# A weight sum in a tile of its own for the second quad of an up-projection on Trainium2

## Chip, core and metric

The kernel runs on one core of one Trainium2 chip. The metric is the device time of one execution in microseconds (us); the time given for a kernel is the median of several executions. TensorE (PE) multiplies, ScalarE (ACT) and VectorE (DVE) prepare and finish tiles, GpSimd (POOL) and SyncE (SP) issue the transfers (DMAs) that matter here; a transfer that adds to what its target holds (accumulating) is issued by POOL, a plain load by SP.

## The reference

One decoder layer on 512 tokens of width 1024, in float32. The part around the change is its last third, a gated MLP with hidden width 2816:

```python
def conv_gated_mlp(x, w_up, conv_w, conv_b, w_down):
    h = x @ w_up                                   # 512x1024 @ 1024x5632
    h = causal_depthwise_conv(h, conv_w, conv_b)   # width 3
    gate, val = jnp.split(h, 2, axis=-1)
    return (jax.nn.silu(gate) * val) @ w_down      # 512x2816 @ 2816x1024

# in the layer, after the mixers (SSD and forgetting attention) and their output projection:
hf = rms_norm(x, norm_ffn_w)
x = x + conv_gated_mlp(hf, w_up, ffn_conv_w, ffn_conv_b, w_down)
```

## The kernel before

**Products.** Every float32 operand is split into a high part (`wh`, `uh`, `sh`, rounded to the multiplier's format) and a low part (`wl`, `ul`, `sl`, what is left), and a product is three matmuls: high by high, high by low, low by high (`mm3`, line 110). A weight tile of 128x1024 is split by one cast on ACT and one subtraction on DVE (`split_up`, line 929); TensorE reads the results.

**Quads.** The up-projection is cut into 11 quads. A quad is 512 output columns: four quarters B11, B12, B21, B22 of the weights, each 128x1024 float32 (512 KB), by two halves of the tokens (H1, H2). Quad 0 is computed plainly (`plain`, `tokens`). From quad 1 on, seven products do the work of eight. Product 0 (`n0`) multiplies B11, product 2 (`n2`) B11+B12, product 3 (`n3`, the fourth) B11+B12+B22, product 4 (`n4`) the sum of all four, product 1 B21, product 5 B22, product 6 B22+B12. One product is 24 matmuls with 256 columns.

**Sums of weights.** They are made by transfers. SP loads B11 into the tile `Ta` (`load_a`, line 995). When it has been split for product 0, POOL adds B12 to it (`more`, line 985, an accumulating transfer); when that has been split for product 2, POOL adds B22; after the split for product 3, B21. So `Ta` holds the four sums one after another, and each addition waits for the split of the sum before it. `Tb` is likewise B22 for product 5 and then B22+B12 for product 6. B21 comes into a tile `wraw` (`Tb` lies in buffers of the same tag). Tiles of tag `T` lie in a pool of two buffers, used in turn, except for every third quad, whose `Ta` has a buffer of its own.

**Quad 1 is special.** It is set up while quad 0 is still being computed, before the loop over `quad_step` starts. Its `Ta` is loaded and gets B12 at once (lines 1352 to 1356); product 0 reads B11 from a second copy, `T0` (line 1358). Then stand, in code order, products 0, 1, 2, 5, the weights of product 0 of quad 2, the weights and product 3, and the weights of product 6. `quad_step(1)` follows: it computes what is left of quad 1 (products 6 and 4) together with products 0, 2, 1, 5 and 3 of quad 2.

**Order.** Each engine and each queue runs its instructions strictly in order; a waiting instruction holds those behind it. The order is set when the kernel is built, by a scheduler with priorities and by explicit "not before" dependencies (`in_turn`, `ordered`, `issue_after`). An accumulating transfer that adds to a tile waits, on POOL, until the earlier transfer into that tile has landed.

**After product 3** ACT copies its result out of PSUM (`n3_kept`, tile `y3`, line 979), since product 6 adds to the same bank. In ACT's order the cast for product 6 (of `Tb`) stands ahead of this copy, and the cast for product 2 of quad 2 behind it.

Of the kernel before, what the change touches and what calls it, by code (L numbers as in the profile page):

```python
# [8 lines left out]
F32 = mybir.dt.float32  # L9
# [6 lines left out]
P = 128  # L16
# [23 lines left out]
def tile_hybrid_layer(  # L40
# [18 lines left out]
    nc = tc.nc  # L59
# [15 lines left out]
    def raw(ap):  # L75
        return ap.bitcast(F32)
# [727 lines left out]
    B11, B12, B21, B22 = 0, 1, 2, 3  # L804
    ADD, SUB = ALU.add, ALU.subtract

    ptt = ctx.enter_context(tc.tile_pool(name="ptt", bufs=1, side="right", reuse_waits="tile"))
# [111 lines left out]
    def ordered(high, low):  # L919
        for name, ins, first in zip(("h", "l"), (high, low()), taken.get(made[0] - 4, (None, None))):  # L920
            in_turn(name, ins)
            if first is not None:
                dep = mybir.DependencyInfo(mybir.DependencyClass.NoSync, mybir.DependencyReason.DATA)
                tc.add_manual_dep(ins.ins, first.ins.name, dep, reason="issue_after")
        made[0] += 1

    def split_up(r, where=None):
        h, l = where or [wp.tile([P, 1024], F32R, tag=t, name=t, bufs=3) for t in ("wh", "wl")]
        ordered(act.copy(h, r), lambda: dve.tensor_tensor(out=l, in0=r, in1=raw(h), op=SUB))  # L929
        return h, l  # L930
# [5 lines left out]
    def pair(n):  # L936
        if FROM[n] not in pairs:
            return None
        pairs[n] = pairs.pop(FROM[n])
        return pairs[n]  # L940
# [7 lines left out]
    quads = [Quad() for _ in range(NH)]  # L948
# [35 lines left out]
    def more(t, quarter, q):  # L984
        last_more[0] = nc.gpsimd.dma_start(t, wup[quarter, q], accum_op=ALU.add)  # L985
# [24 lines left out]
    def n2_weights(q):  # L1010
        u = quads[q]
        u.w2 = split_up(u.ta, pair("n2"))
        more(u.ta, B22, q)

    def n3_weights(q):
        u = quads[q]
        u.w3 = split_up(u.ta, pair("n3"))
        more(u.ta, B21, q)

    def n4_weights(q):  # L1020
        quads[q].w4 = split_up(quads[q].ta, pair("n4"))
# [20 lines left out]
    def n0(q, where=None):  # L1042
        if not hasattr(quads[q], "w0"):
            n0_weights(q, where)
        n0_product(q)
        with urgent():
            n0_kept(q)
# [25 lines left out]
    def n2(q):  # L1073
        n2_weights(q)
        n2_product(q)
        with urgent():
            n2_kept(q)
# [8 lines left out]
    def n3(q):  # L1086
        n3_weights(q)
        n3_product(q)
        with urgent():
            n3_kept(q)  # L1090
# [124 lines left out]
    T = []  # L1215
# [23 lines left out]
    def quad_step(q, ahead=None):  # L1239
# [8 lines left out]
        dve_turn(n1_added(q))  # L1248
        dve_turn(low12(q))
        n2_weights(n)  # L1250
        n0_kept(n)
        n5_weights(n)
# [18 lines left out]
        gate_bias(q)  # L1271
        gate_taps(q, 0)
        n3_weights(n)
        n1_product(n)
        gate_taps(q, 1)
# [10 lines left out]
    def spare():  # L1286
        return [pa.tile([P, 1024], F32R, tag=t, name=t, bufs=1) for t in ("wh", "wl")]
# [68 lines left out]
    tc.add_manual_dep(last_more[0].ins, normed.ins.name, dep, reason="issue_after")  # L1356
    quads[1].t0 = ptt.tile([P, 1024], F32, tag="T", name="T0", bufs=2)
    nc.sync.dma_start(quads[1].t0, wup[B11, 1])
    tokens(1)
    n0(1, spare())  # L1360
    n1_weights(1)
# [5 lines left out]
    pairs.update(n2=four[0], n4=four[3], n1=four[1], n5=four[2])  # L1367
    n0_weights(2)
    n3_weights(1)
    n3_product(1)  # L1370
    n6_weights(1)
# [17 lines left out]
    q = NH - 1  # L1389
# [278 lines left out]
```

## Time and profile before

| | |
|---|---|
| median of 3 runs | 762.45 us (761.83, 762.45, 769.46) |
| profiled execution, its own time | 762.75 us |
| span of the profiled execution | 761.0 us |
| PE busy | 754.4 us (99% of the span) |
| DVE, ACT, POOL busy | 599.3, 487.9, 204.4 us |
| DMA, mean rate over the span | 148 GB/s, 112.91 MB |

The span is from the first to the last instruction; 1.75 us of the profiled execution's own time lie outside it. Times in rows are us from the span's start. A row of the timeline gives start, duration, engine, line, operation, output and input, the count of instructions that were merged into it, and in brackets how long the engine sat idle before it and what ended that. The weights of quad 1 are made from 420 to 485 us; quads 1 to 9 then pass in steps of about 19 us up to 650 us, and the down-projection ends the kernel.

### The profile page before, as it was taken

Reading aid. Unit: us, or ns where it says so; the run is one execution under the profiler, and the core shown is the slowest. Engines: PE = TensorE matmul, PEld = TensorE weight load, DVE = VectorE, ACT = ScalarE, POOL = GpSimd, SP = SyncE. Lnnn points to the kernel's source line nnn. Section 1 sums busy time; section 2 is a strip of 40 time slices with the busy share of each in tenths; the row PEclk is TensorE's granted clock in tenths of the full one; section 3 lists DMA queues with packets and bytes.
Section 4 is the critical chain, followed back from the end, with each engine's and each line's share of the span. In section 5 each row is a group of like instructions: output and inputs, shape, how many; then the busy total and the mean of one; then the engine's idle time right before and its main releaser. Section 6 shows DMA issues by size and latency. Waiting matters only on the chain.

```text
span 761.0 us, 12538 instructions
## 1 busy us (share of the span) xinstructions
PE 754.4 (99%) x4647; PEld 652.2 (86%) x4647; DVE 599.3 (79%) x965; ACT 487.9 (64%) x870; POOL 204.4 (27%) x254
## 2 busy tenths in 40 slices
PE   9999999999999999999999999999999999999997
PEld 7888888887888778787777899999999999888886
DVE  5797788578577676579695787988888888999885
ACT  6655767764379687685673665766666666666551
POOL 0001013445273553134200011333333333223120
PEclk9999999999999999999999999999999999999999
DMA  9534233242254242434221437888888888689992
GB/s 334 181 107 148 84 111 113 83 139 83 85 166 137 58 153 81 127 108 143 84 83 57 166 64 153 193 198 194 194 193 196 193 195 193 179 225 210 252 184 92
DMA packets 35085, 112.91 MB, mean 148 GB/s; under 512 B 4176, under 2 KB 5264, under 8 KB 35024
## 3 DMA queue, kind: packets, MB, share of 16 engines
q1 hardware_dynamic: 23744, 73.58, 28.6%
q0 software_dynamic: 10848, 38.02, 27.4%
q8 instruction: 36, 0.59, 0.3%
q10 hardware_dynamic: 432, 0.52, 0.2%
q14 instruction: 25, 0.20, 0.1%
HBM read 106.24 MB, written 2.20 MB: 142 GB/s over the span
## 4 chain that ended last, share of the span: by engine, by line
PE 98%; DMA 1%; DVE 1%; SPq 0%; issue 0%; ACT 0%; DVEq 0%
PE G L110 19%; PE pw L110 17%; PE g L110 13%; PE Z L110 13%; PE po L110 12%; PE Y L110 5%; PE X L110 4%; PE o L687 2%; PE pT L674 2%; PE y L501 2%; PE j L110 1%; PE S L652 1%; PE S L651 1%; PE qkT L601 1%; DMA wr<-in_wxbc_dram 1%; PE st L523 1%
## 5 line engine op out<-in xcount | busy, mean ns | idle before, releaser
L110 PE MATMUL pw<-wl,xh 128*128 128x512 f32 x192 | 75.8, 395 | 0.0
L110 PE MATMUL pw<-wh,xh 128*128 128x512 f32 x192 | 75.5, 397 | 0.0
L110 PE MATMUL pw<-wh,xl 128*128 128x512 f32 x192 | 75.4, 394 | 0.0
L97 DVE TENSOR_TENSOR wl<-wraw,wh 128x1024 fp32r<-128x1024 f32 x51 | 63.4, 1246 | 8.8 <-ACT wh L96 8.6
L110 PE MATMUL G<-uh,wh 128*128 128x256 f32 x256 | 70.3, 276 | 0.0
L110 PE MATMUL G<-ul,wh 128*128 128x256 f32 x256 | 70.3, 276 | 0.0
L110 PE MATMUL G<-uh,wl 128*128 128x256 f32 x256 | 69.2, 276 | 0.0
L96 ACT CAST wh<-wraw 128x1024 fp32r<-128x1024 f32 x51 | 53.7, 1056 | 14.1 <-PE g L110 5.4
L110 PE MATMUL g<-xh,wh 128*128 128x512 f32 x144 | 56.7, 393 | 0.7 <-ACT wh L188 0.7
L110 PE MATMUL g<-xl,wh 128*128 128x512 f32 x144 | 56.8, 394 | 0.0
L110 PE MATMUL g<-xh,wl 128*128 128x512 f32 x144 | 56.5, 393 | 0.0
L985 POOL DMA_DIRECT2D Ta<-in_wup_dram x30 | 26.2, 875 | 108.6 <-DVE wl L929 106.2
L657 ACT ACTIVATE prob<-prob,nm 128x128 f32<-128x128 f32 (+1 forms) x64 | 35.8, 561 | 27.9 <-DVE nm L653 27.6
L653 DVE CUSTOM_DVE_ANT_0 prob<-S,prob 128x128 f32<-128x128 f32 (+1 forms) x64 | 30.0, 486 | 27.6 <-PE S L652 27.4
L1236 ACT CAST wh<-T 128x1024 fp32r<-128x1024 f32 (+1 forms) x32 | 31.5, 985 | 29.9 <-DMA T<-in_wdown_dram 8.0
L110 PEld LDWEIGHTS G<-ul,wh 128*128 128x128 f32 x256 | 48.1, 188 | 0.0
L110 PEld LDWEIGHTS G<-uh,wh 128*128 128x128 f32 x256 | 48.1, 188 | 0.0
L929 DVE TENSOR_TENSOR wl<-Ta,wh 128x1024 fp32r<-128x1024 f32 x39 | 47.4, 1217 | 0.7 <-ACT wh L929 0.6
L110 PEld LDWEIGHTS G<-uh,wl 128*128 128x128 f32 x256 | 47.4, 188 | 0.0
L1236 DVE TENSOR_TENSOR wl<-T,wh 128x1024 fp32r<-128x1024 f32 (+1 forms) x32 | 36.4, 1137 | 11.5 <-ACT wh L1236 11.4
L110 PE MATMUL G<-sh,wh 128*128 128x256 f32 x160 | 44.2, 276 | 0.0
L110 PE MATMUL G<-sl,wh 128*128 128x256 f32 x160 | 44.2, 276 | 0.0
(305 smaller groups left out, 2421.1 us busy)
## 6 DMA issues: line engine op xcount, KB each, us to landing
Ta<-in_wup_dram POOLq DMA_DIRECT2D x30, 512.0 KB, 5.5
T<-in_wdown_dram POOLq DMA_DIRECT2D x23, 512.0 KB, 7.1
wraw<-in_wqk_dram SPq DMA_DIRECT2D x16, 512.0 KB, 3.6
wraw<-in_wout_dram SPq DMA_DIRECT2D x16, 512.0 KB, 3.3
wraw<-in_wup_dram SPq DMA_DIRECT2D x12, 512.0 KB, 5.0
wraw<-in_wxbc_dram SPq DMA_DIRECT2D x11, 512.0 KB, 3.5
Ta<-in_wup_dram SPq DMA_DIRECT2D x10, 512.0 KB, 7.0
Tb<-in_wup_dram SPq DMA_DIRECT2D x10, 512.0 KB, 6.6
```

The lines of the kernel that those rows point to most:

```text
L96: act.copy(h, r)
L97: dve.tensor_tensor(out=l, in0=r, in1=raw(h), op=ALU.subtract)
L110: ins = pe.matmul(o, a, b, start=start and n == 0, stop=stop and n == 2, **kw)
L501: ins = pe.matmul(o[rows, j * P : (j + 1) * P], w[:, h * HD : (h + 1) * HD], m[:, h, :], start=start and j == 0, stop=stop and j == 3, ski ...
L523: pe.matmul(st, b_tok[:, c, :], x_tok[c], start=True, stop=True)
L653: dve.tensor_tensor_reduce(out=p, in0=sps[:, :n], in1=p, scale=-1.0, scalar=-NEG, op0=ALU.add, op1=ALU.min, accum_out=nm[:, qb : qb + 1],)
L657: act.activation(p, p, AF.Exp, scale=-1.0, bias=nm[:, qb : qb + 1], accum_out=sm[:, qb : qb + 1])
L674: pe.transpose(t[:, w : w + P], prob[:, o : o + P], ident)
L687: ins = pe.matmul(o[rows, kb * P :], v[:, kb, (2 * pair + i) % 8, :], pt[:, w : w + SEQ - kb * P], start=kb == 0, stop=kb == NTB - 1, skip ...
L929: ordered(act.copy(h, r), lambda: dve.tensor_tensor(out=l, in0=r, in1=raw(h), op=SUB))
L985: last_more[0] = nc.gpsimd.dma_start(t, wup[quarter, q], accum_op=ALU.add)
L1236: ordered(act.copy(hs, src[:, :n]), lambda: dve.tensor_tensor(out=ls, in0=src[:, :n], in1=raw(hs), op=SUB))
```

## The change

Quad 1 gets a tile `T3` of its own for B11+B12+B22, in the second buffer of tag `T`. SP loads B11 into it, and POOL adds B12 and B22 to it one behind the other. `Ta` of quad 1 no longer stands still at that sum: after the split for product 2, POOL adds B22 and then B21 at once. Other quads are unchanged. The work of one load (512 KB) and two accumulating transfers is added, and none is removed.

```diff
     def n2_weights(q):
         u = quads[q]
         u.w2 = split_up(u.ta, pair("n2"))
         more(u.ta, B22, q)
+        if hasattr(u, "t3"):
+            more(u.ta, B21, q)
 
     def n3_weights(q):
         u = quads[q]
-        u.w3 = split_up(u.ta, pair("n3"))
-        more(u.ta, B21, q)
+        u.w3 = split_up(getattr(u, "t3", u.ta), pair("n3"))
+        if not hasattr(u, "t3"):
+            more(u.ta, B21, q)
...
     quads[1].t0 = ptt.tile([P, 1024], F32, tag="T", name="T0", bufs=2)
     nc.sync.dma_start(quads[1].t0, wup[B11, 1])
+    quads[1].t3 = ptt.tile([P, 1024], F32, tag="T", name="T3", bufs=2)
+    nc.sync.dma_start(quads[1].t3, wup[B11, 1])
+    for quarter in (B12, B22):
+        more(quads[1].t3, quarter, 1)
     tokens(1)
     n0(1, spare())
```

The order of the matmuls on PE is the same before and after. On POOL, the place is that of the first accumulating transfers of the up-projection. `Ta_4618` is `Ta` of quad 1, `Ta_4851` that of quad 2 (`Ta_4856` in the change), `Tb_4812` and `Tb_4949` are `Tb` of quads 1 and 2 (`Tb_4817`, `Tb_4953`). Before:

```order
L985 DMA Ta_4618<-in_wup_dram 128x1024 x2
L985 DMA Tb_4812<-in_wup_dram 128x1024
L985 DMA Ta_4851<-in_wup_dram 128x1024
L985 DMA Ta_4618<-in_wup_dram 128x1024
L985 DMA Ta_4851<-in_wup_dram 128x1024
L985 DMA Tb_4949<-in_wup_dram 128x1024
```

And with the change:

```order
L985 DMA Ta_4618<-in_wup_dram 128x1024
L985 DMA T3_4623<-in_wup_dram 128x1024 x2
L985 DMA Ta_4618<-in_wup_dram 128x1024 x2
L985 DMA Tb_4817<-in_wup_dram 128x1024
L985 DMA Ta_4856<-in_wup_dram 128x1024 x2
L985 DMA Tb_4953<-in_wup_dram 128x1024
```

The two additions to `T3` stand ahead of B22 for `Ta` of quad 1. The addition of B21 to that `Ta` has moved from behind B12 for `Ta` of quad 2 to ahead of B12 for `Tb` of quad 1.

On SP, the place is that of the loads around `T0`. `Ta_4913` (`Ta_4917` in the change) is `Ta` of quad 3, `wraw_4956` (`wraw_4960`) holds B21 of quad 3, `wraw_4983` (`wraw_4987`) B21 of quad 2, which goes into the buffer that `Tb` of quad 1 leaves. Before:

```order
L1358 DMA T0_4621<-in_wup_dram 128x1024
L995 DMA Ta_4851<-in_wup_dram 128x1024
L995 DMA Ta_4913<-in_wup_dram 128x1024
L989 DMA wraw_4956<-in_wup_dram 128x1024
L989 DMA wraw_4983<-in_wup_dram 128x1024
```

And with the change:

```order
L1361 DMA T0_4621<-in_wup_dram 128x1024
L1363 DMA T3_4623<-in_wup_dram 128x1024
L995 DMA Ta_4856<-in_wup_dram 128x1024
L989 DMA wraw_4960<-in_wup_dram 128x1024
L995 DMA Ta_4917<-in_wup_dram 128x1024
L989 DMA wraw_4987<-in_wup_dram 128x1024
```

`T3` takes the buffer and the place that `Ta` of quad 2 had; `Ta` of quad 2 takes the place and the buffer of `Ta` of quad 3, which in turn waits for the split of `T3` and stands behind `wraw_4960`.

On ACT, the place is that of the casts that read these tiles; its order is unchanged but for the source of the second row. With the change:

```order
L929 CAST wh_4848<-Ta_4856 128x1024
L929 CAST wh_4854<-T3_4623 128x1024
L979 COPY z2_4815<-Z_4790 128x512
L1171 ACTIVATE ua_4907<-ua_4907 128x512
L1171 ACTIVATE ua_4909<-ua_4909 128x512
L929 CAST wh_4850<-Tb_4817 128x1024
L979 COPY y3_4944<-G_4727 128x512
L929 CAST wh_4852<-Ta_4856 128x1024
```

The rows are, in order, the splits for product 0 of quad 2 and product 3 of quad 1, a copy, two activations of quad 0, the split for product 6 of quad 1, the copy `y3`, and the split for product 2 of quad 2. Before, the second row reads `Ta_4618`.

## Prediction

> **What bounds the kernel now.** I read first the page's busy times, then its chain of work that ended last, then the waits of TensorE (engine, line and what it waited for: us in total, times, longest).
>
> ```profile
> PE 754.4 (99%) x4647; PEld 652.2 (86%) x4647; DVE 599.3 (79%) x965; ACT 487.9 (64%) x870; POOL 204.4 (27%) x254
> PE 98%; DMA 1%; DVE 1%; SPq 0%; issue 0%; ACT 0%; DVEq 0%
> PE g L219 <- DVE misc L141: 1.0, 1, 1.0
> PE g L110 <- ACT wh L188: 0.7, 1, 0.7
> PE po L110 <- DVE x L278: 0.3, 1, 0.3
> ```
>
> TensorE is busy in all but 761.0 - 754.4 = 6.6 us, and its waits come to 2.0 us, none in the up-projection. The chain is TensorE. So nothing that the change speeds up off TensorE can be worth more than 6.6 us (0.9%), and what it speeds up in the up-projection is worth nothing, since TensorE waits for nothing there. What remains to ask is whether the added transfers make TensorE wait. For that I need its deadlines, and what stands in ACT and DVE ahead of them.
>
> ```profile
> 476.99 0.28 PE L110 MATMUL G<-sh,wh 128*128 128x256 f32 x1
> 477.21 0.28 PE L110 MATMUL G<-sh,wl 128*128 128x256 f32 x1
> 479.93 0.28 PE L110 MATMUL Z<-uh,wl 128*128 128x256 f32 x1
> 485.26 0.39 PE L110 MATMUL G<-uh,wl 128*128 128x256 f32 x2
> 490.81 0.28 PE L110 MATMUL G<-sh,wl 128*128 128x256 f32 x1
> 466.19 2.00 ACT L929 CAST wh<-Ta 128x1024 fp32r<-128x1024 f32 x2 [2.02 <-PE Z L110]
> 469.68 1.05 ACT L929 CAST wh<-Tb 128x1024 fp32r<-128x1024 f32 x1
> 475.26 0.59 ACT L979 COPY y<-G 128x512 f32<-128x512 f32 x1 [4.53 <-PE G L110]
> 475.74 1.05 ACT L929 CAST wh<-Ta 128x1024 fp32r<-128x1024 f32 x1
> 479.06 1.05 ACT L929 CAST wh<-Ta 128x1024 fp32r<-128x1024 f32 x1 [0.34 <-DMA Ta<-in_wup_dram]
> 480.02 1.05 ACT L929 CAST wh<-wraw 128x1024 fp32r<-128x1024 f32 x1
> 467.28 2.36 DVE L929 TENSOR_TENSOR wl<-Ta,wh 128x1024 fp32r<-128x1024 f32 x2
> 470.77 1.23 DVE L929 TENSOR_TENSOR wl<-Tb,wh 128x1024 fp32r<-128x1024 f32 x1 [1.12 <-ACT wh L929]
> 477.09 1.22 DVE L929 TENSOR_TENSOR wl<-Ta,wh 128x1024 fp32r<-128x1024 f32 x1
> 488.96 1.21 DVE L929 TENSOR_TENSOR wl<-Ta,wh 128x1024 fp32r<-128x1024 f32 x1
> ```
>
> Product 6 of quad 1 begins at 476.99, and its third matmul, at 477.21, is the first to read the low part. The same place of product 2 of quad 2 is 479.93, of product 1 of quad 2 the second matmul of the 485.26 row (485.38), of product 3 of quad 2 490.81. A split takes from the cast's start to the low part's end 470.77 + 1.23 - 469.68 = 2.32 us. The cast of `Tb` therefore has to start by 477.21 - 2.32 = 474.9 and that of `Ta` of quad 2 (475.74) by 477.6: slacks of 5.2 and 1.9 us.
>
> **The change part by part.** The transfers of before, as issued: SP's loads (`Ta` of quads 2 and 3, B21 of quad 3, B21 of quad 2), then POOL's additions (B22 to `Ta` of quad 1, B12 to its `Tb`, B12 to `Ta` of quad 2, B21 to `Ta` of quad 1).
>
> ```profile
> 443.55 0.33 SPq L995 DMA_DIRECT2D Ta<-in_wup_dram  x1
> 454.86 0.33 SPq L995 DMA_DIRECT2D Ta<-in_wup_dram  x1
> 456.00 0.33 SPq L989 DMA_DIRECT2D wraw<-in_wup_dram  x1
> 472.02 0.33 SPq L989 DMA_DIRECT2D wraw<-in_wup_dram  x1
> 459.93 0.88 POOL L985 DMA_DIRECT2D Ta<-in_wup_dram  x1 [15.94 <-DVE wl L929]
> 464.34 0.86 POOL L985 DMA_DIRECT2D Tb<-in_wup_dram  x1 [3.53 <-DVE wl L929]
> 468.92 0.87 POOL L985 DMA_DIRECT2D Ta<-in_wup_dram  x1 [3.71 <-DVE wl L929]
> 470.07 0.87 POOL L985 DMA_DIRECT2D Ta<-in_wup_dram  x1 [0.28 <-issue]
> ```
>
> Their times from issue to landing (the last number), of the loads issued at 443.55, 456.00 and 472.02, then of the four additions:
>
> ```profile
> Ta<-in_wup_dram SPq DMA_DIRECT2D x1, 512.0 KB, 4.6
> wraw<-in_wup_dram SPq DMA_DIRECT2D x1, 512.0 KB, 4.1
> wraw<-in_wup_dram SPq DMA_DIRECT2D x1, 512.0 KB, 7.6
> Ta<-in_wup_dram POOLq DMA_DIRECT2D x1, 512.0 KB, 5.4
> Tb<-in_wup_dram POOLq DMA_DIRECT2D x1, 512.0 KB, 5.3
> Ta<-in_wup_dram POOLq DMA_DIRECT2D x1, 512.0 KB, 5.7
> Ta<-in_wup_dram POOLq DMA_DIRECT2D x1, 512.0 KB, 9.0
> ```
>
> And the load on the DMA engines by stretch (the number ahead of GB/s is their busy share):
>
> ```profile
> 450.00:455.00 5.00, 5.00 (x44) 5.00 (x44) 3.88 (x6) 3.51 (x6) 0.00 (x0) 1.00 0.00 0
> 455.00:460.00 5.00, 5.00 (x46) 5.00 (x45) 5.00 (x7) 4.00 (x7) 0.07 (x1) 1.00 0.63 213
> 460.00:465.00 5.00, 5.00 (x47) 5.00 (x46) 5.00 (x8) 2.98 (x4) 1.47 (x2) 1.00 0.64 105
> 475.00:480.00 5.00, 5.00 (x46) 5.00 (x46) 3.65 (x4) 4.01 (x5) 0.86 (x1) 1.00 0.59 164
> 480.00:499.00 19.00, 19.00 (x170) 19.00 (x170) 16.80 (x22) 12.85 (x18) 6.04 (x6) 1.00 0.93 197
> ```
>
> From 460 to 465 one addition runs alone: 0.64 x 5 = 3.2 us of the engines, within 5.4 us from issue to landing.
>
> *T3 itself.* Its load takes the place of 443.55 and lands at 443.55 + 4.6 = 448.2. Its two additions, each waiting on POOL for the transfer before it, end at 448.2 + 5.4 = 453.6 and at about 459.0, or near 462 if the two loads of 454.86 and 456.00 run beside the second. The engines stood idle from 450 to 455. Product 3's cast is the second of the merged ACT row (466.19, so about 467.1), behind a cast that TensorE releases: `T3` is ready 5 us early, and the cast gains nothing from it. In before, B22 landed at 459.93 + 5.4 = 465.3, also in time. What the change takes away was no wait.
>
> *Ta of quad 1.* B22 is issued at 459.93 as before, since the DVE split releases it. B21 follows on its landing, at 465.4 instead of 470.07. Product 4's split waits 0.34 us for it in before (the 479.06 row); that wait goes, and TensorE did not feel it.
>
> *Tb of quad 1, and what it is moved past.* B12 for `Tb` was issued at 464.34. Now it stands behind B21 for `Ta`, which holds POOL until 465.4, and spaced by 1.15 us as 470.07 stands to 468.92: 466.55. Its landing is not in the trace; the bounds are 5.3 us (464.34, alone) and 9.0 us (470.07, the second of two additions 1.15 us apart with a load issued beside them 2 us later). I take 9.0, since here too a load comes beside it: `Ta` of quad 3, which now waits for `T3`'s split (the second of the merged DVE row 467.28 + 2.36) and starts near 469.7. So `Tb` is ready at 475.55 instead of 469.68. The cast has been due since 469.7; it ends its split at 475.55 + 2.32 = 477.87, which **holds TensorE 0.7 us** at 477.21. The copy `y3` behind it ends at 477.1, against 476.99, within that.
>
> *Ta of quad 2.* Its B12 is still issued at 468.92, but as the third addition in the queue: 3.2 us of engine time after `Tb`'s, so landing at 478.75 (before: 474.6; bounds 475.05, if `Tb` takes 5.3, and 478.75 here). Split done at 481.07, due at 479.93: **1.15 us in all**.
>
> *B21 of quad 2.* It goes into `Tb`'s buffer, so its load moves from 472.02 to 477.9. Bounds 4.1 and 7.6 us; I take 4.1, since the additions ahead are nearly through by then and the next come only after the late split. It lands at 482.0, just when ACT comes to that cast (478.75 and about 3.4 us of casts and copy), 2.1 us later than the 480.02 row. By then DVE is 2.2 us late. It is nearly full until product 3's low part of quad 2, which ended at 488.96 + 1.21 = 490.17, a slack of 0.64 us. At 492.4 against 490.81: **1.6 us in all**. With 7.6 us instead, product 1's low part comes at 487.8 against 485.38 (2.4 us), and product 3's about 4.3 us late, 3.7 us in all.
>
> After that I count nothing: DVE works 16.80 of the 19 us from 480 to 499, so it regains some 2 us a quad.
>
> Sum: 0 removed, 1.6 us added, on the profiled execution's own 762.75 us (span 761.0): 764.4 us. The median shown lies 0.3 us lower, hence **764.1 us**. The ends: 0 us, if the additions take 5.3 us; 5.2 us, if `Ta`'s B22 also takes 9.0 (then `Tb` is ready at 479.15, `Ta` of quad 2 at 482.35, and DVE 5.8 us late at 490.17).
>
> [...]
>
> **The rivals.** *Hidden* (762.5 us): the additions land in 5.3 to 5.7 us each even in threes; `Tb` at 471.9, `Ta` of quad 2 at 475.1, both before 474.9 and 477.6. For it: the first of the 468.92 pair took 5.7. Against: the second took 9.0. *A larger stall* (765.5 to 767.7): `Ta`'s B22 is slowed by the tail of `T3`'s, or B21 of quad 2 takes 7.6. *A backlog that stays* (slower by over 1%): a quad's DMA work is four additions of 3.2 us and three loads of about 1.6 us (half of the 0.63 x 5 = 3.15 busy us that two loads make from 455 to 460), 17.6 us, in 19.04 us of TensorE (seven products of 2.72 us, from 477.21 to 479.93). It decides at 19.04 us: if additions in company cost 3.6 us, each quad falls back further, and nine quads at 0.85 us make 7.6 us. Against it: the share is 0.93, not 1, and 475 to 480 has 2 us idle for the 2.2 us that I count as left over. *The change does nothing at its place* is true of product 3 in any case; it is the same time as *hidden*. *Faster by over 1%* has no room in 6.6 us of idle time, noise aside.
>
> **How the numbers follow.** Stall of 0.5 to 3 us, 0.60; hidden, 0.25; larger, 0.08; lasting backlog, 0.05; faster, 0.02. A measurement of this kernel tells about 1% from no change. So: within 1% 0.93, slower by more 0.05, faster by more 0.02. The range goes from the lower runs of before (hidden, 761.83) to the larger stall, 761.5 to 767.0.
>
> **What would show it.** In the changed profile POOL's row for `Tb` stands near 466.5 instead of 464.3; the cast of `Tb` waits on a DMA until about 475.5, that of `Ta` of quad 2 until 478.7; TensorE has waits on DVE's `wl` of about 1 us in 477 to 492, and the rest of the up-projection is the same, shifted. I am wrong if ACT's cast of `Tb` still starts before 475 (then hidden), or if waits of TensorE recur in each quad up to 650 us (then backlog).

## Result, and the profile after

| | before | changed |
|---|---|---|
| median | 763.27 us (22 runs) | 767.66 us (22 runs, 765.01 to 774.30) |
| ratio to before, over all runs | 1 | 1.007, 95% interval 1.0043 to 1.0096 |
| profiled execution, its span | 761.0 us | 765.3 us |

The change makes the kernel slower, by 0.7% over all runs; the two medians lie 0.58% apart. The runs of either kernel fall into two groups some 6.5 us apart, in different shares (see the last section), and the lower groups alone have medians of 763.06 us (18 runs) and 766.99 us (12 runs), 3.9 us apart. A second set of runs gave 766.51 us and 1.0049 (1.0032 to 1.0065):

> The changed kernel once more, on the chip of the other runs of this set: 767.7 us, a wait of 3.1 us at product 6 and a slow clock of about 3.3 us behind it. [...]

Six of its runs lie from 765.3 to 768.1 us; the seventh, the profiled one, took 4348 us, and its trace is not used here. The mean granted clock is 1.0 in three of the six and 0.996 or 0.997 in the other three; the medians of the two threes are 765.82 and 766.51 us.

The waits of TensorE in the changed kernel's profile:

```profile
PE G L110 <- DVE G L1057: 3.1, 1, 3.1
PE g L219 <- DVE misc L141: 1.0, 1, 1.0
PE g L227 <- ACT xh L193: 0.6, 1, 0.6
PE X L110 <- DVE wl L1239: 0.4, 1, 0.4
PE po L110 <- DVE x L278: 0.3, 1, 0.3
```

One is new in the up-projection, of 3.1 us, and it is for DVE's sum in G (line 1057, `n1_added`), not for the low part of a split. The chain to it, on POOL, ACT, DVE and TensorE:

```profile
453.90 0.86 POOL L985 DMA_DIRECT2D T<-in_wup_dram  x1 [5.06 <-DMA T<-in_wup_dram]
458.80 0.87 POOL L985 DMA_DIRECT2D Ta<-in_wup_dram  x1 [4.04 <-DVE wl L929]
466.22 0.87 POOL L985 DMA_DIRECT2D Ta<-in_wup_dram  x1 [6.55 <-DMA Ta<-in_wup_dram]
466.96 1.02 POOL L985 DMA_DIRECT2D Tb<-in_wup_dram  x1
467.79 1.07 POOL L985 DMA_DIRECT2D Ta<-in_wup_dram  x1
462.46 0.59 ACT L979 COPY y<-G 128x512 f32<-128x512 f32 x1 [0.44 <-PE G L110]
476.17 1.04 ACT L929 CAST wh<-Tb 128x1024 fp32r<-128x1024 f32 x1 [7.57 <-DMA Tb<-in_wup_dram]
479.22 1.05 ACT L929 CAST wh<-Ta 128x1024 fp32r<-128x1024 f32 x1 [1.52 <-DMA Ta<-in_wup_dram]
477.25 1.23 DVE L929 TENSOR_TENSOR wl<-Tb,wh 128x1024 fp32r<-128x1024 f32 x1 [8.73 <-ACT wh L929]
478.39 0.69 DVE L1057 TENSOR_TENSOR G<-G,y 128x512 f32<-128x512 f32 x1
475.75 0.28 PE L110 MATMUL G<-uh,wl 128*128 128x256 f32 x1
479.13 0.58 PE L110 MATMUL G<-sh,wh 128*128 128x256 f32 x1 [3.11 <-DVE G L1057]
483.52 0.28 PE L110 MATMUL Z<-uh,wh 128*128 128x256 f32 x1
```

Of before, the same copy `y0` of quad 1, the sum in G, and the first matmul of product 2 of quad 2:

```profile
463.59 0.59 ACT L979 COPY y<-G 128x512 f32<-128x512 f32 x1 [0.44 <-PE G L110]
475.88 0.70 DVE L1054 TENSOR_TENSOR G<-G,y 128x512 f32<-128x512 f32 x1 [3.89 <-ACT y L979]
479.71 0.28 PE L110 MATMUL Z<-uh,wh 128*128 128x256 f32 x1
```

By the copy, the changed profile runs 1.13 us ahead of that of before up to this place (462.46 against 463.59), so 1.1 is to be added where times are compared.

POOL waits 6.55 us for the landing of B22 in `Ta`, issues B21 behind it, and only then B12 for `Tb`, which could have gone at about 463 (the split that releases it is done then). Times to landing of these transfers: the second addition to `T3`, then the four that follow.

```profile
T<-in_wup_dram POOLq DMA_DIRECT2D x1, 512.0 KB, 9.4
Ta<-in_wup_dram POOLq DMA_DIRECT2D x1, 512.0 KB, 7.0
Ta<-in_wup_dram POOLq DMA_DIRECT2D x1, 512.0 KB, 5.4
Tb<-in_wup_dram POOLq DMA_DIRECT2D x1, 512.0 KB, 9.1
Ta<-in_wup_dram POOLq DMA_DIRECT2D x1, 512.0 KB, 11.4
```

`Tb` lands 9.1 us after 466.96, at 476.1. Its split and the sum behind it end at 479.08, and product 6 starts at 479.13. TensorE would have been free at 475.87 (475.75 and one step of 0.12): it stood 3.26 us. Then product 6 takes 4.39 us (479.13 to 483.52) where a product takes 2.72. The stretches of that time show why (the number behind the POOL column is the granted clock):

```profile
476.00:479.00 3.00, 0.03 (x1) 0.00 (x0) 1.75 (x3) 1.53 (x2) 0.00 (x0) 1.00 0.65 128
479.00:480.00 1.00, 0.86 (x4) 0.87 (x5) 0.68 (x2) 0.78 (x1) 0.00 (x0) 0.53 0.27 74
481.00:482.00 1.00, 1.00 (x7) 1.00 (x6) 0.79 (x2) 1.00 (x2) 0.07 (x1) 0.50 0.20 78
482.00:483.00 1.00, 1.00 (x9) 1.00 (x8) 1.00 (x2) 0.64 (x1) 0.80 (x1) 0.76 0.00 0
483.00:484.00 1.00, 1.00 (x12) 1.00 (x11) 1.00 (x1) 0.35 (x1) 0.64 (x1) 1.00 0.27 20
```

The clock falls to half as TensorE starts again, at 479.06 (a mean of 0.53 from 479 to 480), and is back at 482.48 (0.76 from 482 to 483), 3.4 us later. So 3.26 us of standing and 1.67 us of slow clock are lost at one place: 4.93 us. Less the 1.13 us that this profile was ahead, the rest of the up-projection runs 3.81 us later than in before (483.52 against 479.71), and another 0.5 us goes in the down-projection and the end: 765.3 against 761.0.

The slow clock did not come in every execution. Half a clock for 3.4 us takes 0.002 (1.7 of 765 us) off the mean granted clock of an execution, and the profiled one has 0.998. Of the twelve lower runs of the changed kernel seven have 0.996 to 0.998, and five have 0.999 or 1.0, too much for such a stretch; the medians are 767.09 and 766.22 us.

### The profile page after: what moved, and what is told of

Read it like the earlier page. It is cut to its first block, busy times and chain, and to the rows that moved or that the text cites. A ratio compares the mean times of both kernels' runs of the same rounds, so it can differ in the third digit from the quotient of the medians.

```text
span 765.3 us, 12542 instructions
## 1 busy us (share of the span) xinstructions
PE 755.2 (99%) x4647; PEld 653.3 (85%) x4647; DVE 599.1 (78%) x965; ACT 487.8 (64%) x870; POOL 204.9 (27%) x256
## 4 chain that ended last, share of the span: by engine, by line
PE 86%; issue 5%; DMA 3%; DVE 2%; POOL 2%; ACT 1%; DVEq 0%; SPq 0%; POOLq 0%; ACTq 0%
PE pw L110 17%; PE G L110 17%; PE g L110 13%; PE po L110 12%; PE Z L110 8%; PE Y L110 3%; PE o L687 2%; PE pT L674 2%; PE y L501 2%; PE X L110 2%; PE j L110 1%; PE S L652 1%; PE S L651 1%; POOL T L1228 1%; DMA T<-in_wdown_dram 1%
```

## The experiments

My theory was the **queue order**: `Tb`'s addition stands on POOL behind one that waits for a landing. The rival was the **traffic**: one load and two additions more make every transfer late, in whatever order.

**B21 of `Ta` behind B12 of `Tb`** (e2_tb_first). All added transfers stay; one is moved.

```diff
     def n2_weights(q):
...
-        if hasattr(u, "t3"):
-            more(u.ta, B21, q)
...
     def n5_weights(q):
...
         more(u.tb, B12, q)
+        if hasattr(u, "t3"):
+            with tc.issue_after(last_more[0].ins):
+                more(u.ta, B21, q)
```

> As the changed kernel, but on GpSimd's queue the addition of B21 to Ta of quad 1 stands behind the addition of B12 to its Tb. All added transfers remain. Theory 'queue order' (Tb's addition was late because it stood behind one that waits for a landing): Tb's B12 is issued at 463.2 us instead of 467.0 and lands by about 469 (the landing of Ta's B22 at 465.8 and 3.2 us of engine time), product 6 of quad 1 waits for nothing, the clock stays at 1.0, and the time is that of before (763.3 us) within 1 us. Ta of quad 2 may still land near 477, which would cost up to 0.5 us. Rival 'traffic' (the 8 us of added engine time make every addition late, in whatever order): Tb lands after 474.5 all the same, product 6 waits 1.5 us or more, 765 us or more.

Measured: 763.22 us, ratio 1.0001 (0.998 to 1.0022). On POOL, and the waits of TensorE from 440 to 640 us:

```profile
464.17 0.87 POOL L985 DMA_DIRECT2D Tb<-in_wup_dram  x1 [3.45 <-DVE wl L929]
PE Z L110 <- ACT wh L929: 0.3, 1, 0.3
PE G L110 <- DVE Z L1112: 0.2, 1, 0.2
```

`Tb`'s addition is issued when its split allows and lands 7.0 us later, product 6 waits for nothing, and what remains is 0.5 us of small waits behind the `Ta` of quads 2 and 3. The same traffic in another order costs nothing that the measurement shows (the lower groups have 762.94 and 763.04 us). The traffic is not the cause by itself.

**B21 of `Ta` last** (e1_b21_late), behind B12 of quad 2's `Ta`, as in before; `T3` stays.

```diff
     def n2_weights(q):
...
-        if hasattr(u, "t3"):
-            more(u.ta, B21, q)
...
     def n3_weights(q):
         u = quads[q]
         u.w3 = split_up(getattr(u, "t3", u.ta), pair("n3"))
-        if not hasattr(u, "t3"):
+        if hasattr(u, "t3"):
+            with tc.issue_after(last_more[0].ins):
+                more(u.ta, B21, q)
+        else:
             more(u.ta, B21, q)
```

> As the changed kernel, but B21 goes to Ta of quad 1 where it stood before, as the last of the four additions (behind B12 for Ta of quad 2). T3 and its load and two additions remain. Queue order: Tb's B12 at 463.2, Ta of quad 2 at 467.8, B21 near 469 and landed near 477, just in time for product 4; no wait of TensorE, 763.3 us within 1 us. Traffic: TensorE waits 1.5 us or more in the up-projection, 765 us or more.

Measured: 767.51 us, 1.0051 (1.002 to 1.0081), but in two groups: six runs of twelve from 763.3 to 765.2, six from 769.9 to 773.3. Its profile (span 763.4) is of the lower group: product 6 waits for nothing, `Ta` of quad 1 lands at 480.1 instead of 477, and about 1 us is lost behind it, which I had not expected. The lower group (median 763.81) agrees with the queue order within that; the upper one neither theory had (see the last section).

**Less on `T3`.** One addition (e3_one_add), and none (e7_no_add); the queue order is the change's. The edit is that of e3; e7 leaves the loop out.

```diff
-    for quarter in (B12, B22):
+    for quarter in (B12,):
         more(quads[1].t3, quarter, 1)
```

> As the changed kernel, but T3 gets one addition (B12) instead of two; the kernel leaves B22 out of product 3 of quad 1. The order on the queue stays. Queue order: Ta's B22 lands without the tail of T3's second addition, 5.4 us after 458.8 instead of 7.0, so Tb's B12 is issued near 465.1 and lands 9.1 us later at 474.2; with 2.9 us from the cast's start to the end of DVE's sum in G, product 6 can start at 477.1 instead of 475.9: a wait of 1.2 us, no slow clock, 764.5 us. Traffic: with 3.2 us of 8 gone the loss falls in proportion, to about 3 us (766.3), slow clock included.

> As the changed kernel, but T3 gets no addition at all (the kernel leaves B12 and B22 out of product 3 of quad 1): one load is all the traffic that is added, the order of the other additions is that of the change. Queue order: as with one addition, a wait of about 1.2 us at product 6 and 764.5 us, since Ta's B22 runs alone in both. Traffic: nothing is left of the loss, 763.3 us.

Measured: e3 772.2 us, 1.0115 (1.0098 to 1.0132), all five runs from 770 to 774; e7 766.0 us, 1.0059 (1.0033 to 1.0084), seven runs from 764.3 to 766.6 and four from 771.0 to 773.1. The casts of `Tb` and of quad 2's `Ta` in e7:

```profile
473.31 1.05 ACT L929 CAST wh<-Tb 128x1024 fp32r<-128x1024 f32 x1 [3.69 <-DMA Tb<-in_wup_dram]
479.50 1.04 ACT L929 CAST wh<-Ta 128x1024 fp32r<-128x1024 f32 x1 [3.75 <-DMA Ta<-in_wup_dram]
```

With no addition to `T3` at all, `Tb` is still 3.6 us later than the 469.68 of before and quad 2's `Ta` 3.8 us later than 475.74. At product 6 this costs less than the 1.2 us that I had expected: TensorE stops for 0.6 us there in e3, and in e7 not at all, whose product 6 runs from 476.88 to its last matmul at 479.49 without a gap. The stops come behind it, at products 2 and 1 of quad 2, where I had expected none. In e7:

```profile
479.49 0.28 PE L110 MATMUL G<-sh,wl 128*128 128x256 f32 x1
480.60 0.38 PE L110 MATMUL Z<-uh,wh 128*128 128x256 f32 x1 [0.83 <-ACT wh L929]
481.86 0.39 PE L110 MATMUL Z<-uh,wl 128*128 128x256 f32 x1 [0.76 <-DVE wl L929]
485.03 0.38 PE L110 MATMUL G<-uh,wh 128*128 128x256 f32 x1 [0.16 <-DVE Z L1111]
```

Against an even step of 0.113 us from matmul to matmul, TensorE loses 2.4 us here in e3 and 2.6 us in e7, in stops of at most 1.0 us, with the clock at 1.00. So the order with a single load more costs 2.6 us of the 4.93. The additions to `T3` add the rest: one alone adds nothing in e3's profile, and with both there is one stop of 3.26 us, behind which the clock falls. Traffic as the rival put it (nothing left in e7) falls, but under the change's order it adds nearly as much again. The run times say the same where they can be compared: the lower group of e7 has 765.28 us, 2.2 above that of its before, against 3.9 for the change. Those of e3 are all at the slower pace of the last section, so its 772.2 bears out neither of the times that were expected.

**A late `Tb` without `T3`** (e9_before_late_tb): the kernel before, B12 of `Tb` moved behind the other two.

```diff
     def n3_weights(q):
...
         more(u.ta, B21, q)
+        if q == 1:
+            with tc.issue_after(last_more[0].ins):
+                more(u.tb, B12, q)
```

(`n5_weights` leaves it out for quad 1.)

> The kernel before, with no T3, but the addition of B12 to Tb of quad 1 stands behind those to Ta of quad 2 and to Ta of quad 1 (B21): no transfer is added, one is late. Queue order: it is issued near 471.2 and lands about 9 us later at 480.2, DVE's sum in G ends 2.9 us after that, and product 6 waits 6 us from 477.0, then runs slow for 1.7 us: about 771 us. Traffic: no traffic is added, 763.3 us.

Measured: 770.49 us, 1.011 (1.0093 to 1.0127). One wait in the up-projection, and the clock behind it:

```profile
PE Z L110 <- ACT wh L929: 5.7, 1, 5.7
480.00:482.00 2.00, 0.24 (x1) 0.24 (x2) 1.69 (x2) 1.71 (x3) 0.00 (x0) 0.56 0.01 4
482.00:484.00 2.00, 2.00 (x10) 2.00 (x11) 2.00 (x4) 1.77 (x3) 0.00 (x0) 0.50 0.64 211
484.00:486.00 2.00, 2.00 (x12) 2.00 (x11) 2.00 (x2) 0.71 (x1) 1.43 (x2) 0.50 0.34 74
486.00:488.00 2.00, 2.00 (x15) 2.00 (x15) 0.65 (x2) 0.56 (x1) 0.28 (x1) 0.73 0.96 162
```

No transfer is added, one is late, and the loss is larger than the change's, as the queue order has it. The clock is at half from 480.2 to 487.1, 6.8 us and not 3.4, so this part of the loss was more than I expected. (The scheduler put two matmuls of product 2 of quad 2 ahead of product 6 here, hence the name in the wait.)

**Filling the gap** (e4_fill, then e4b_fill): 26 matmuls (`FILL`) into a part of PSUM, the memory that takes TensorE's results, that nobody reads yet, ahead of product 6. The edit is that of e4b.

```diff
+        if q == 1:
+            quads[n].Z = two_banks("Z", "Z")
+            with tc.issue_after(last_product[0].ins):
+                for k in range(FILL):
+                    filled = pe.matmul(
+                        quads[n].Z[:, k % 2, H2], up_operand(4)[0][:, 0, 0:P], up_operand(4)[0][:, k % 4],
+                        start=True, stop=True, skip_group_check=True,
+                    )
+            with tc.issue_after(filled.ins):
+                n6_product(q)
```

> As the changed kernel, but with 26 matmuls of 256 columns ahead of product 6 of quad 1, whose results nobody reads: they fill 2.95 of the 3.26 us that TensorE sat idle there. Theory 'clock' (the 1.67 us that product 6 takes longer than 2.72 us come from the granted clock, which fell to 0.5 after the idle gap): the clock stays at 1.0, product 6 takes 2.7 us, and the time is 1.7 us below the changed kernel's, about 766.0. Rival (product 6 is slow because its operands arrive slowly, or its memory is disturbed by the transfers): product 6 still takes 4.4 us, and the time is unchanged at 767.7.

The first form read weights of product 3, in a tile that is filled anew for quad 2 by then; so the fill itself waited 5.3 us for that later cast, ran at a clock of 0.5, and says nothing on product 6 (775.55 us, 1.0184, 1.0151 to 1.0217). The second reads tokens:

> The fill once more, now with operands that were ready long before: 26 matmuls of 256 columns between the last product ahead of the gap and product 6 of quad 1, results read by nobody. Theory 'clock' (product 6 took 4.39 us instead of 2.72 because the granted clock fell to 0.5 after 3.3 us without a matmul): the gap shrinks to about 0.3 us, the clock stays at 1.0, product 6 takes 2.7 us, and quad 1 to 9 run 1.7 us earlier against the changed kernel's profile; 765 to 766 us in runs at 2.72 us a product. Rival (product 6 is slow because its operands arrive late one by one): it still takes over 4 us.

```profile
478.00:479.00 1.00, 1.00 (x10) 1.00 (x10) 1.00 (x2) 0.00 (x0) 0.00 (x0) 1.00 0.34 57
481.00:482.00 1.00, 1.00 (x11) 1.00 (x10) 0.90 (x1) 1.00 (x3) 0.00 (x0) 1.00 0.42 168
480.21 0.28 PE L111 MATMUL G<-sh,wh 128*128 128x256 f32 x1
483.04 0.28 PE L111 MATMUL Z<-uh,wh 128*128 128x256 f32 x1
```

The clock stays at 1.00, product 6 takes 2.83 us, and product 2 starts 1.72 us earlier than in the changed kernel (this profile is 1.24 us behind it up to there: 483.04 - 1.24 = 481.80 against 483.52). The clock theory holds. The time does not follow: 773.71 us, 1.0132 (1.0111 to 1.0154), since from the fill on every product takes 2.83 us. Whether the fill brings that pace on is not shown.

**The split behind the sums** (e5_split_behind, e5b_split_behind): `n6_weights(1)` moved into `quad_step(1)`, behind `n1_added` and `low12`.

> As the changed kernel, but the split for product 6 of quad 1 stands behind the copy y3 and DVE's two sums on ACT and DVE, instead of ahead of them. Theory 'sum in G' (product 6's first matmul waits for DVE's sum in G, which stood behind the split): the sums are done near 475.5, product 6 starts on its high part near 477.2 and gets the low part near 478.5, so about 2.4 us are lost instead of 4.9, with no slow clock: 765.3 us. Rival (product 6 waits for the split itself): it starts no earlier than before, and 4 us or more are lost.

Inconclusive: the scheduler again put two matmuls of product 2 of quad 2 ahead of the rest of product 6, and they waited 3.0 us for quad 2's `Ta` (773.31 us, 1.0129, 1.0098 to 1.0161). With these held behind product 6:

> The split for product 6 of quad 1 behind the copy y3 and DVE's two sums, and the matmuls of product 2 of quad 2 held behind product 6, so that TensorE's order is that of the change. Theory 'sum in G': product 6's first matmul can start when the high part is there, near 477.2 where quad 1's copy stands at 463.5, and its low part comes near 478.5; about 2.5 us are lost at product 6 and the clock stays at 1.0, against 4.9 us in the changed kernel. Then Ta of quad 2 is next and may hold product 2 near 480. Rival (the split itself is waited for): 4 us or more are lost at product 6.

```profile
PE G L110 <- ACT wh L929: 2.5, 1, 2.5
PE G L110 <- DVE wl L929: 0.8, 1, 0.8
480.00:482.00 2.00, 1.34 (x11) 1.34 (x12) 0.88 (x2) 1.35 (x2) 0.00 (x0) 0.96 0.25 49
478.30 1.04 ACT L929 CAST wh<-Tb 128x1024 fp32r<-128x1024 f32 x1 [2.67 <-DMA Tb<-in_wup_dram]
479.40 0.38 PE L110 MATMUL G<-sh,wh 128*128 128x256 f32 x1 [2.47 <-ACT wh L929]
475.66 0.70 DVE L1057 TENSOR_TENSOR G<-G,y 128x512 f32<-128x512 f32 x1 [6.24 <-ACT y L979]
```

With the sum out of the way, product 6's first matmul waits for the high part alone, and starts 1.1 us after the cast's start (478.30) instead of 2.96 us: the sum in G was what held it. The gain is eaten otherwise: `Tb` landed about 1.2 us later than in the change's profile, and the clock fell all the same: not in the stops of 2.64 and 0.93 us, but at 481.84 (0.96 from 480 to 482), when TensorE had been issuing again for 1.2 us, and for 3.4 us. The median is 768.06 us, 1.0082 (1.0059 to 1.0106), 5.1 us above its before where I had expected some 2.5.

**One stop in the kernel before** (e10_stop): product 4 of quad 1 waits for ACT.

> The kernel before, with no transfer added or moved, but the first matmul of product 4 of quad 1 waits for an activation on ACT that ends near 483.5, so TensorE stops once for about 1.0 us. Theory 'pace is drawn at a stop' (a product takes 2.72 or 2.83 us; which of the two holds from one stop to the next): the kernel loses 1.0 us in some runs (764 us) and 6.6 us more in others (770 to 771), more of them than in the kernel before. Rival (the slow pace comes from the added transfers): 764 us in nearly all runs.

Measured: 766.39 us, 1.006 (1.0037 to 1.0083); five runs from 765.7 to 767.0, one 771.3. Holding product 4 also delayed what follows on DVE: the profile has stops of about 0.3 and 1.4 us, so more was lost than meant. The pace stayed at 2.72 us a product in the profile; one run in six is no evidence that a stop alone brings the slow pace.

## Why the prediction was wrong

**Right.** TensorE is the bound and the change has nothing to win: product 3's cast starts at 466.02 in the changed profile, 1.1 us ahead like all else there, so it gained nothing. The place, the chain (B21 ahead of `Tb`'s B12 on POOL, the cast of `Tb`, product 6), and the sign of the stall were as described. No backlog stayed from quad to quad. The measured 767.66 lies 0.66 us above the range, in the upper end of the rival *a larger stall* (765.5 to 767.7), to which I had given 0.08 and whose top the range left out; one of its two conditions, `Ta`'s B22 slowed by the tail of `T3`'s, is what came. That the time lies so near the range is partly luck: errors in both directions stand below, and the median holds ten runs at a slower pace that the prediction did not know of. Also, 0.8 us of the distance from the forecast is its base, 762.45 us from three runs, where 22 give 763.27.

**Wrong, the step on `Tb`, in its size.** This is the step of the sum that failed: the stall at product 6 was put at 0.7 us; it is 3.26. Two parts. First, B22 of `Ta` was priced at 5.4 us and took 7.0, as the second addition to `T3` was still in flight (9.4 us, beside two loads; in e3 and e7, without it, POOL's next row comes 5.5 and 5.6 us behind that issue, here 7.4); with that POOL's row for `Tb`, forecast near 466.5, stands at 466.96, which is 468.1 in before's time, and `Tb` came 1.6 us later than forecast (476.1 and 1.1 against 475.55). I had this as the upper end and not as the value, though I had written myself that `T3`'s second addition might last to 462. Second, the deadline was wrong: I let product 6 wait for the low part at its third matmul, 2.32 us after the cast's start. Its first matmul waits for DVE's sum in G, which stands behind that split on DVE: 2.92 us after the cast's start, and 0.22 us earlier on TensorE, 0.8 us in all. In before, DVE's 475.88 row for that sum was in the trace, and ended 0.4 us ahead of product 6; I had followed the weights only.

**Wrong, a term left out: the clock.** Behind the stop of 3.26 us the granted clock fell to 0.5, 1.67 us more in the profiled execution, and e4b, where TensorE does not stop, keeps it at 1.00. My sum had no term for it. The half clock lasts 3.4 us in the changed kernel and in e5b, and twice that, 6.8 us, in e9; e3 and e7, with no stop over 1.0 us, have none. By their mean clock, five of the twelve lower runs of the changed kernel had no such stretch; and in e5b the clock fell behind stops of 2.64 and 0.93 us, with TensorE at work again for 1.2 us. What sets the 3.4 us is not shown. How much idle time it takes stays open.

**Wrong the other way: the later steps.** Product 2 and product 3 of quad 2 were to add 0.45 us each. In the changed kernel they add nothing, since the one large stop makes TensorE later than quad 2's `Ta`. In e7, where product 6 does not stop, products 2 and 1 of quad 2 do add, 2.6 us, since a third addition in line took 10.7 to 11.4 us to land (e7, the change), where I had added 3.2 us to the second.

**Two prices.** An addition of 512 KB was priced at 5.3 to 9.0 us from issue to landing; those named here took from 5.1 us (B21 of `Ta` in e7) to 11.4 (the changed kernel, behind others in flight). And the backlog rival was priced wrongly: four additions of 3.6 us and three loads of 1.6 us make 19.2 us, which is 0.16 us over 19.04 and not 0.85, so its condition gives 1.4 us in nine quads and not 7.6.

## What to carry to other kernels

Before a transfer is put on a queue in which its predecessor must land first, list what stands behind it there and when that is due: here one addition moved two places forward, beside one load and two additions more, cost 0.7%, and moved back behind the urgent one it cost nothing that the measurement shows, with the same traffic. Take the deadline from everything that the waiting engine's first instruction needs, sums in the same PSUM tile too, not only its weights. A stop of TensorE cost more than its length here: behind stops of 2.64 (e5b) to 5.9 us (e9) the profiles have 3.4 or 6.8 us of half clock, behind those of up to 1.4 us (e10) alone none.

## What the runs showed of the hardware

**Two paces at full clock.** A product of 24 matmuls takes either 2.72 or 2.83 us, with the granted clock at 1.00 in both, and keeps one of the two for hundreds of matmuls. The rows are matmuls of one form from 520 to 560 us (the last number but one is the mean ns of one), and stretches of 20 us, of before and then of e2_tb_first:

```profile
L110 PE MATMUL G<-uh,wh 128*128 128x256 f32 x53 | 14.5, 276 | 0.0
520.00:540.00 20.00, 20.00 (x178) 20.00 (x178) 17.66 (x22) 13.80 (x19) 6.06 (x6) 1.00 0.91 195
```

```profile
L110 PE MATMUL G<-uh,wh 128*128 128x256 f32 x48 | 13.4, 281 | 0.0
520.00:540.00 20.00, 20.00 (x172) 20.00 (x171) 17.04 (x22) 12.90 (x18) 6.04 (x6) 1.00 0.81 184
```

178 matmuls against 172 in the same time. Seven products at 0.11 us make some 0.8 us a quad and 6.9 us over nine quads, which is about the distance between the two groups of runs of one kernel. Before had 18 runs of 22 from 761.8 to 764.0 and four from 769.5 to 770.3; the changed kernel had twelve from 765.0 to 767.7 and ten from 771.1 to 774.3. The medians and ratios above mix them. e2's profile (768.0 us) is at the slower pace, though its median equals that of before. The profiles of e2, e3, e4b and e7, whose profiled runs lie in the upper groups, are at 2.83 us a product; those of before, the change, e1 and e10, whose profiled runs lie in the lower groups, at 2.72.

In the profiles of e2, e3 and e7 the pace changes for good at a stop of TensorE of 0.3 to 0.6 us; in that of e4b it changes with the first matmuls of the fill, without a stop. A stop does not always do it (the changed kernel's profile and e10's kept 2.72 us after theirs), and no run of before at the slower pace was profiled. What chooses the pace stays open. The changed kernel had it in ten of 22 runs and then in none of six, which shows how far such shares can be trusted.
